# A hybrid attention and RWKV-7 block with experts: paired chunk products, later value products and row maxima by way of DRAM in the mixer stage

## The chip, the cores and the metric

The kernel runs on one core of a Trainium2 chip. Times are device microseconds of one execution; the time before is the median of three runs. A core has a matmul engine (TensorE, PE in the profile; its weight loads stand apart as PEld), VectorE (DVE), ScalarE (ACT), GpSimd (POOL) and SyncE (SP), which here issues nearly all transfers. PE writes its results to PSUM, which has eight banks of 512 fp32 per partition; DVE and ACT read them from there.

## The reference, cut to what matters

One encoder block over 2048 tokens of width 1024, in fp32:

```
p = rmsnorm(x) (modulated) @ w_in
o_att  = softmax(q k^T / 8) v      8 heads of 64 on 2 key/value heads, all 2048 keys
o_rwkv = for each direction, per token:
           sa = S (-kk);  S = S*w + sa (kk*a)^T + v k^T;  y = S r    8 heads, S is 64x64
x = x + gate * (concat(o_att, o_rwkv) @ w_out)
x = x + gate * (16 expert FFNs, each on its 256 best tokens)
```

The change is in the two token mixers alone, `o_att` and `o_rwkv`. In the attention each row of scores has its maximum subtracted before the exponential, and the weighted values are divided by the row's sum. RWKV's recurrence is computed in chunks of 64 tokens: for each head and chunk there are 64x64 products of the chunk's columns with each other, masked to one triangle; a triangular system is solved for them; and then the state is carried from chunk to chunk.

## The kernel before, in words

Four stages follow one another: the projections with their preparation, the mixers, the output projection with the router, and the experts. Instructions are issued in an order that is decided when the kernel is built: a scheduler simulates the engines, and at each moment takes the earliest instruction in program order that is ready; `high_priority` lets a block go ahead of what stands before it. On the chip each engine then keeps to its list, SP's transfers too: an instruction that must wait holds up everything behind it on its engine.

In the mixers (`mixers`) two generators are stepped in turn. `attention` goes through 16 blocks, a block being a pair of heads j and a quarter qc of 512 queries. Within a block (`att_out`) 16 key blocks of 128 follow each other: four matmuls give the scores of two heads (L694, L695) in the one two-bank buffer `st`, ACT takes the exponential (L696), DVE and POOL add it to the running sums (L699), and `values` multiplies it by the values (L686), the two heads side by side in the left and right 64 columns of the array. fp32 matmuls are two instructions each in the trace, fp32r ones one. At every second key block the value products of the two key blocks before it are issued at high priority. One step of a key block also takes three steps of `att_max` for the next block: 32 score tiles (L647, L648), reduced by DVE (L649) in two PSUM buffers `s`, then the maxima are split in a high and a low part (L654, L655), eight small matmuls with the identity turn them into rows (L660) and two ACT copies put them in rows 64 and 65 of the tile `qa` (L662), so that the score matmuls of that block subtract them. After a block `att_finish` sums over the partitions (L669), takes the reciprocal (L671) and multiplies.

`rwkv` goes through 16 groups (4 head pairs, 2 directions, 2 halves of the sequence), each of four quarters of four chunk pairs. For a quarter `rw_a1` loads a tile `xin` and, for each head, multiplies 64 rows of it by each other in four matmuls into one PSUM tile (L846); DVE masks the tile (L849); four transposes and an ACT copy follow (L854, L855), and two transfers bring the parts that the solve needs to DRAM (L857). These tiles all use PSUM bank `pa`, except that group 1 goes round `pa`, `pb` and `pc`. `rw_solve` loads the 32x32 diagonal blocks back (L867) and solves them in 30 dependent steps on DVE or POOL (L876, L878), writes them to DRAM (L886), and `rw_merge` joins them with matmuls (L915, L921). The recurrence itself (`rq_av`, `rq_wu`, `rq_l`, `rq_step`: L955 to L1011) uses banks `pb` and `pc`. In `rwkv` each quarter has four stations; `extra` runs at each of them and takes one step of `rw_a1` for the group after next, three of the solve, and one of the finish. A group's `rw_a1` has twelve steps, so that it ends with the third quarter of the group that runs.

Of the kernel before, what the change touches and what calls it, by code (L numbers as in the profile page):

```python
# [7 lines left out]
F32 = mybir.dt.float32  # L8
F32R = mybir.dt.float32r
# [580 lines left out]
class Attention(Encoder):  # L590
    def attention_pools(self, c):
# [9 lines left out]
        self.kl1 = self.a_k.tile([66, T], F32R, name="kl1")  # L601

# [19 lines left out]
    def att_max(self, j, qc, keys, res):  # L622
# [30 lines left out]
        hl = self.a_q.tile([P, 8, 2], F32R, tag="mhl", name="mhl")  # L653
        nc.vector.tensor_copy(out=hl[:, :, 0], in_=nm)  # L654
        nc.vector.tensor_tensor(out=hl[:, :, 1], in0=nm, in1=hl[:, :, 0].bitcast(F32), op=ALU.subtract)  # L655
        yield
        for h in range(2):
            pm = self.a_ps.tile([P, 512], F32, tag="s", name="m_ps", bufs=SB)
            for qt in range(4):
                nc.tensor.matmul(pm[64:66, qt * P : (qt + 1) * P], hl[:, 4 * h + qt, :].bitcast(F32), self.ident,  # L660
                                 start=True, stop=True, tile_position=(0, 64))
            nc.scalar.copy(out=q2[h][64:66, :], in_=pm[64:66, :])  # L662
            yield

    def att_finish(self, j, qc, av, acc):
# [5 lines left out]
        nc.vector.reciprocal(out=rec, in_=sm)  # L671
# [3 lines left out]
    def att_out(self, keys, v, q):  # L675
# [12 lines left out]
        for kb in range(16):  # L688
# [4 lines left out]
            for h in range(2):  # L693
                nc.tensor.matmul(s[:, h, :], khh[:, ks], qs[h], start=True, stop=False)  # L694
                nc.tensor.matmul(s[:, h, :], kl1[:, ks], q2[h], start=False, stop=True)  # L695
# [7 lines left out]
            if kb % 2 == 0 and kb:  # L703
                with self.tc.high_priority():
# [61 lines left out]
class Rwkv(Attention):  # L766
# [59 lines left out]
    def rw_a1(self, n, g):  # L826
# [5 lines left out]
        banks = cycle(("pa", "pb", "pc") if n == 1 else ("pa",))  # L832
        mask = self.masks[d]
        for i0, q in enumerate(range(4) if d == 0 else range(3, -1, -1)):
# [5 lines left out]
            rv = r56.rearrange("p c (x k) -> p c x k", k=64)  # L840
            for h in range(2):
                hs = slice(64 * h, 64 * h + 64)
                p1 = self.bank(next(banks)).tile([P, 4, P], F32, tag="p", name="p1")
                for i in range(4):
                    xr, u = X[hs, i // 2, :], i % 2
                    nc.tensor.matmul(p1[:, i, :].rearrange("p (x k) -> p x k", k=64), xr[:, 128 * u : 128 * u + 128],  # L846
                                     xr[:, 256:512].rearrange("p (x u k) -> p x u k", x=2, u=2)[:, :, u, :], start=True, stop=True)
                dst = rv[:, :, 0:3:2, :] if h == 0 else rv[:, :, 3:5, :]
                nc.vector.tensor_tensor(out=dst, in0=p1.rearrange("p c (x k) -> p c x k", k=64),  # L849
                                        in1=mask.unsqueeze(1).to_broadcast([P, 4, 2, 64]), op=ALU.mult)  # L850
                yield
# [763 lines left out]
```

## Time and profile before

| what | value |
|---|---|
| time, median of 3 runs | 3756.29 us (3753.66 to 3756.6) |
| the profiled execution's own time | 3751.49 us |
| its span from first to last instruction | 3749.8 us |
| PE busy over the span | 3509.9 us (94%) |
| DVE, ACT, POOL busy | 2516.7, 1755.2, 1512.5 us (67%, 47%, 40%) |
| granted PE clock, mean of the span | 0.957 of full |

The page gives shares over the whole span, in which the stages have different limits. The mixers alone fill PE from about 860 us to 2340 us; the projections lie before and the output projection, the router and the experts behind. "Busy" of PE contains modelled ends of matmuls, so that the distance from the start of one group of matmuls to the start of the next is the safer measure of what it costs.

### The profile page before, as it was taken

How to read it: one execution, taken by the hardware profiler on the slowest of the kernel's cores; microseconds unless marked ns; L12 is line 12 of the kernel's file. 1: busy time of each engine (PE TensorE's matmuls, PEld its weight loads, DVE VectorE, ACT ScalarE, POOL GpSimd, SP SyncE). 2: the span in 40 equal slices, each digit the busy share in tenths (PEclk: the TensorE clock that was granted, in tenths of full speed). 3: DMA queues.
4: the chain of work that ended last, by engine and by line, in shares of the span. 5: the costliest groups of instructions: out<-in, count | busy, mean ns of one | idle time of the engine just before them, and what ended most of it. 6: DMA issues, size and time to landing. Idle time of an engine off the chain costs nothing. (4 is left out here: it accounts for less than half of the span.)

```text
span 3749.8 us, 61495 instructions
## 1 busy us (share of the span) xinstructions
PE 3509.9 (94%) x23436; PEld 2856.7 (76%) x23436; DVE 2516.7 (67%) x4289; ACT 1755.2 (47%) x3066; POOL 1512.5 (40%) x1484
## 2 busy tenths in 40 slices
PE   6998899799999999999999997993999999999998
PEld 5887788656666666676666664772999999999997
DVE  6688778876857778558867675447555656655653
ACT  4445444414555555545555564231444444444443
POOL 3445344526263353663364554332332332322321
PEclk8999899879999999999999998996999999999999
DMA  5335334443323433433333232443566766767664
GB/s 182 105 130 168 112 113 141 139 129 73 91 68 79 121 95 85 114 88 87 84 85 85 69 82 82 156 145 113 188 206 205 222 202 216 218 203 222 220 199 127
DMA packets 531228, 510.93 MB, mean 136 GB/s; under 512 B 213304, under 2 KB 449954, under 8 KB 525812
## 3 DMA queue, kind: packets, MB, share of 16 engines
q1 hardware_dynamic: 520612, 472.08, 41.1%
q0 software_dynamic: 10000, 34.91, 4.0%
q8 instruction: 185, 3.03, 0.3%
q14 instruction: 111, 0.91, 0.1%
q10 hardware_dynamic: 320, 0.00, 0.0%
HBM read 392.57 MB, written 109.07 MB: 134 GB/s over the span
## 5 line engine op out<-in xcount | busy, mean ns | idle before, releaser
L1452 DVE TENSOR_TENSOR w_lo<-w_raw,w_hi 128x2048 fp32r<-128x2048 f32 x189 | 432.3, 2293 | 385.8 <-ACT w_hi L1449 385.4
L1516 PE MATMUL gu<-hh,w_lo 128*128 128x256 f32 x2048 | 573.5, 280 | 0.0
L1516 PE MATMUL gu<-hl,w_hi 128*128 128x256 f32 x2048 | 572.7, 280 | 0.0
L1516 PE MATMUL gu<-hh,w_hi 128*128 128x256 f32 x2048 | 572.5, 280 | 0.0
L699 POOL TENSOR_TENSOR acc<-acc,pt 128x512 f32<-128x512 f32 x256 | 354.9, 1391 | 469.0 <-ACT pt L696 456.0
L1449 ACT CAST w_hi<-w_raw 128x2048 fp32r<-128x2048 f32 x192 | 366.9, 1912 | 319.9 <-PE down L1539 133.3
L696 ACT ACTIVATE pt<-st_ps 128x1024 f32<-128x1024 f32 x256 | 262.2, 1024 | 394.8 <-PE st_ps L695 221.2
L649 DVE TENSOR_REDUCE mx<-s_ps 128x1 f32<-128x512 f32 x512 | 342.6, 681 | 149.7 <-PE s_ps L648 148.2
L247 PE MATMUL proj_ps<-hh,w_hi 128*128 128x258 f32 (+1 forms) x1280 | 375.3, 294 | 32.8 <-DVE s_k L265 23.8
L1516 PEld LDWEIGHTS gu<-hh,w_lo 128*128 128x128 f32 x2048 | 388.0, 189 | 0.0
L1516 PEld LDWEIGHTS gu<-hh,w_hi 128*128 128x128 f32 x2048 | 385.6, 188 | 1.3
L1516 PEld LDWEIGHTS gu<-hl,w_hi 128*128 128x128 f32 x2048 | 385.5, 188 | 1.4
L247 PE MATMUL proj_ps<-hl,w_hi 128*128 128x258 f32 (+1 forms) x1280 | 373.0, 292 | 6.4 <-DVE hl L149 5.9
L247 PE MATMUL proj_ps<-hh,w_lo 128*128 128x258 f32 (+1 forms) x1280 | 371.5, 290 | 0.0
L149 POOL TENSOR_TENSOR dl<-hid,dh 128x256 fp32r<-128x256 f32 x128 | 135.1, 1056 | 448.1 <-ACT dh L148 447.8
L686 PE MATMUL o_ps<-pt,av 128*64 128x512 f32 x1024 | 278.5, 627 | 6.7 <-ACT pt L696 6.7
L247 PEld LDWEIGHTS proj_ps<-hh,w_hi 128*128 128x128 f32 x1280 | 250.8, 196 | 41.7 <-issue 23.0
L247 PEld LDWEIGHTS proj_ps<-hl,w_hi 128*128 128x128 f32 x1280 | 251.4, 196 | 10.6 <-DVE hl L149 6.6
L699 DVE TENSOR_TENSOR acc<-acc,pt 128x512 f32<-128x512 f32 x192 | 194.7, 1014 | 91.0 <-ACT pt L696 90.3
L247 PEld LDWEIGHTS proj_ps<-hh,w_lo 128*128 128x128 f32 x1280 | 250.6, 196 | 2.1 <-issue 1.1
L647 PE MATMUL s_ps<-khh,qhl 128*128 128x512 f32 x512 | 240.6, 471 | 9.5 <-DVE mx L649 8.1
L694 PE MATMUL st_ps<-qhl,khh 128*128 128x512 f32 x512 | 229.0, 447 | 2.8 <-ACT pt L696 1.8
(418 smaller groups left out, 8125.1 us busy)
## 6 DMA issues: line engine op xcount, KB each, us to landing
w_raw<-in_w_gate_dram SPq DMA_DIRECT2D x64, 1024.0 KB
w_raw<-in_w_up_e_dram SPq DMA_DIRECT2D x64, 1024.0 KB
w_raw<-in_w_down_dram SPq DMA_DIRECT2D x64, 1024.0 KB
d_x<-X SPq DMA_DIRECT2D x32, 1024.0 KB
xin<-d_x SPq DMA_DIRECT2D x64, 512.0 KB
w_raw<-in_w_in_dram SPq DMA_DIRECT2D x80, 256.0 KB
mod_w<-in_w_ada_dram SPq DMA_DIRECT2D x64, 256.0 KB
mod_w<-in_w_ada_dram SPq DMA_DIRECT2D x8, 1024.0 KB
```

What stands on the lines that cost most here:

```text
L149: (eng or nc.gpsimd).tensor_tensor(out=lo, in0=src, in1=hi.bitcast(F32), op=ALU.subtract)
L247: nc.tensor.matmul(acc[:, :n], a[:, kt, :], b[:, kt, lo : lo + n], start=(kt == 0 and m == 0), stop=(kt == KT - 1 and m == 2))
L647: nc.tensor.matmul(s, qs[h][:, ts], khh[:, ks], start=True, stop=False)
L649: nc.vector.tensor_reduce(out=mx[:, 4 * h + qt, kc : kc + 1], in_=s, axis=AX.X, op=ALU.max)
L686: nc.tensor.matmul(av[64 * h : 64 * h + 64, :], v[:, kb, :], pt[:, h, :], start=(kb == 0), stop=(kb == 15), tile_position=(0, 64 * h))
L694: nc.tensor.matmul(s[:, h, :], khh[:, ks], qs[h], start=True, stop=False)
L696: nc.scalar.activation(out=pt, in_=s, func=AF.Exp, scale=0.125)
L699: eng.tensor_tensor(out=acc[:, h, :], in0=(first if kb == 1 else acc)[:, h, :], in1=pt[:, h, :], op=ALU.add)
L1449: nc.scalar.copy(out=hi, in_=raw)
L1452: eng.tensor_tensor(out=lo, in0=raw, in1=hi.bitcast(F32), op=ALU.subtract)
L1516: nc.tensor.matmul(acc[:, m, :], a[:, kt, i * P : (i + 1) * P], b[:, kt, :], start=(kt == 0 and n == 0), stop=(kt == KT - 1 and n == 2))
```

## The change

Six edits. In `rw_a1` the two heads' products go to two tiles in banks `pa` and `pb`, and the four matmuls of one head alternate with those of the other, each head's in its own half of the array's rows; masks, transposes and copies are as before, the step between the two heads is gone (so that a group has eight steps instead of twelve), and group 1 no longer uses `pc`. `extra` takes a step of `rw_a1` only at the third and fourth station of a quarter. In `att_out` the value products of two key blocks are ordered behind the last score matmul of the current key block. In `att_max` the split maxima of both heads are turned by one transpose of 16 columns, copied by ACT, written to DRAM, and read back by two transfers into rows 64 and 65 of the two `qa` tiles. In `att_finish` the reciprocal is taken in four parts of 128 columns. In the output projection a gap in SBUF is 512 bytes larger, which follows the new tile's size.

```diff
--- before.py
+++ after.py
@@ -599,6 +599,7 @@
         self.ones = self.a_k.tile([P, 64], F32, name="ones")
         self.nc.vector.memset(self.ones, 1.0)
         self.kl1 = self.a_k.tile([66, T], F32R, name="kl1")
+        self.d_m = self.dram.tile([4, 4, 2, 2, 512], F32, name="d_m")
 
     def att_keys(self, g):
 
@@ -650,17 +651,21 @@
                     yield
         nm = self.a_q.tile([P, 8], F32, tag="nm", name="nm")
         nc.vector.tensor_reduce(out=nm, in_=mx, axis=AX.X, op=ALU.max, negate=True)
-        hl = self.a_q.tile([P, 8, 2], F32R, tag="mhl", name="mhl")
-        nc.vector.tensor_copy(out=hl[:, :, 0], in_=nm)
-        nc.vector.tensor_tensor(out=hl[:, :, 1], in0=nm, in1=hl[:, :, 0].bitcast(F32), op=ALU.subtract)
+        hl = self.a_q.tile([P, 2, 2, 4], F32R, tag="mhl", name="mhl")
+        n3 = nm.rearrange("p (h t) -> p h t", h=2)
+        nc.vector.tensor_copy(out=hl[:, :, 0, :], in_=n3)
+        nc.vector.tensor_tensor(out=hl[:, :, 1, :], in0=n3, in1=hl[:, :, 0, :].bitcast(F32), op=ALU.subtract)
+        yield
+
+        pm = self.a_ps.tile([P, 512], F32, tag="s", name="m_ps", bufs=SB)
+        nc.tensor.transpose(pm[:16, :P], hl.bitcast(F32).rearrange("p h x t -> p (h x t)"), self.ident)
+        mt = self.a_q.tile([16, P], F32, tag="mt", name="mt", bufs=1)
+        nc.scalar.copy(out=mt, in_=pm[:16, :P])
+        nc.sync.dma_start(out=self.d_m[j, qc].rearrange("h x (t p) -> (h x t) p", p=P), in_=mt)
         yield
         for h in range(2):
-            pm = self.a_ps.tile([P, 512], F32, tag="s", name="m_ps", bufs=SB)
-            for qt in range(4):
-                nc.tensor.matmul(pm[64:66, qt * P : (qt + 1) * P], hl[:, 4 * h + qt, :].bitcast(F32), self.ident,
-                                 start=True, stop=True, tile_position=(0, 64))
-            nc.scalar.copy(out=q2[h][64:66, :], in_=pm[64:66, :])
-            yield
+            nc.sync.dma_start(out=q2[h][64:66, :].bitcast(F32), in_=self.d_m[j, qc, h])
+        yield
 
     def att_finish(self, j, qc, av, acc):
         nc = self.nc
@@ -668,7 +673,9 @@
         for h in range(2):
             nc.tensor.matmul(sm[64 * h : 64 * h + 64, :], self.ones[:, 0:64], acc[:, h, :], start=True, stop=True, tile_position=(0, 64 * h))
         rec = self.a_l.tile([P, 512], F32, tag="rec", name="rec")
-        nc.vector.reciprocal(out=rec, in_=sm)
+
+        for c in range(0, 512, P):
+            nc.vector.reciprocal(out=rec[:, c : c + P], in_=sm[:, c : c + P])
         nc.vector.tensor_tensor(out=rec, in0=av, in1=rec, op=ALU.mult)
         (nc.gpsimd if (j, qc) == (3, 3) else nc.sync).dma_start(out=self.d_o[j, :, qc * 512 : (qc + 1) * 512], in_=rec)
 
@@ -692,7 +699,7 @@
             s = self.o_ps.tile([P, 2, 512], F32, tag="st", name="st_ps", bufs=1)
             for h in range(2):
                 nc.tensor.matmul(s[:, h, :], khh[:, ks], qs[h], start=True, stop=False)
-                nc.tensor.matmul(s[:, h, :], kl1[:, ks], q2[h], start=False, stop=True)
+                st = nc.tensor.matmul(s[:, h, :], kl1[:, ks], q2[h], start=False, stop=True)
             nc.scalar.activation(out=pt, in_=s, func=AF.Exp, scale=0.125)
             if kb:
                 for h, eng in enumerate((nc.gpsimd if kb % 8 == 3 else nc.vector, nc.gpsimd)):
@@ -701,7 +708,7 @@
                 first = pt
 
             if kb % 2 == 0 and kb:
-                with self.tc.high_priority():
+                with self.tc.high_priority(), self.tc.issue_after(st.ins):
                     values(kb - 2)
                     values(kb - 1)
             if kb >= 6 and self.block in MOD_BLOCKS:
@@ -755,7 +762,7 @@
         self.att_finish(*done)
 
 
-from itertools import chain, cycle
+from itertools import chain
 
 GC = 16
 QB = 2
@@ -829,7 +836,6 @@
         ct, d, half = g["id"]
         c0 = half * GC
         g["r56"] = {}
-        banks = cycle(("pa", "pb", "pc") if n == 1 else ("pa",))
         mask = self.masks[d]
         for i0, q in enumerate(range(4) if d == 0 else range(3, -1, -1)):
             X = self.r_x.tile([P, 2, 512], F32, tag="xin", name="xin")
@@ -838,18 +844,20 @@
             r56 = self.r56_of(n, i0).tile([P, 4, 384], F32, tag="r56", name="r56")
             g["r56"][q] = r56
             rv = r56.rearrange("p c (x k) -> p c x k", k=64)
+
+            p1 = [self.bank(b).tile([P, 4, P], F32, tag="p", name="p1") for b in ("pa", "pb")]
+            for i in range(4):
+                for h in range(2):
+                    xr, u = X[64 * h : 64 * h + 64, i // 2, :], i % 2
+                    nc.tensor.matmul(p1[h][:, i, :].rearrange("p (x k) -> p x k", k=64), xr[:, 128 * u : 128 * u + 128],
+                                     xr[:, 256:512].rearrange("p (x u k) -> p x u k", x=2, u=2)[:, :, u, :], start=True, stop=True,
+                                     tile_position=(64 * h, 0))
             for h in range(2):
-                hs = slice(64 * h, 64 * h + 64)
-                p1 = self.bank(next(banks)).tile([P, 4, P], F32, tag="p", name="p1")
-                for i in range(4):
-                    xr, u = X[hs, i // 2, :], i % 2
-                    nc.tensor.matmul(p1[:, i, :].rearrange("p (x k) -> p x k", k=64), xr[:, 128 * u : 128 * u + 128],
-                                     xr[:, 256:512].rearrange("p (x u k) -> p x u k", x=2, u=2)[:, :, u, :], start=True, stop=True)
                 dst = rv[:, :, 0:3:2, :] if h == 0 else rv[:, :, 3:5, :]
-                nc.vector.tensor_tensor(out=dst, in0=p1.rearrange("p c (x k) -> p c x k", k=64),
+                nc.vector.tensor_tensor(out=dst, in0=p1[h].rearrange("p c (x k) -> p c x k", k=64),
                                         in1=mask.unsqueeze(1).to_broadcast([P, 4, 2, 64]), op=ALU.mult)
-                yield
-            p2 = self.bank(next(banks)).tile([P, 4, P], F32, tag="p", name="p2")
+            yield
+            p2 = self.bank("pa").tile([P, 4, P], F32, tag="p", name="p2")
             for i in range(4):
                 nc.tensor.transpose(p2[:, i, :], X[:, i // 2, 128 * (i % 2) : 128 * (i % 2) + 128], self.ident)
             nc.scalar.copy(out=rv[:, :, 1:6:4, :], in_=p2.rearrange("p c (x k) -> p c x k", k=64))
@@ -1108,8 +1116,10 @@
                     with self.tc.high_priority():
                         self.rq_step(prev, j)
 
-            def extra():
-                run(a1, 1)
+            def extra(j):
+
+                if j >= 2:
+                    run(a1, 1)
                 if k < 3:
                     run(solve, 3)
                 else:
@@ -1119,14 +1129,14 @@
 
             step(0)
             self.rq_l(Qs[i], 0)
-            extra()
+            extra(0)
             yield
             step(1)
             self.rq_l(Qs[i], 1)
-            extra()
+            extra(1)
             yield
             step(2)
-            extra()
+            extra(2)
             stage_load(i + 2)
             yield
             step(3)
@@ -1134,7 +1144,7 @@
                 fin = chain(fin, self.rq_done(prev, *quarters[i - 1]))
             if i + 2 < len(quarters):
                 self.rq_av(Qs[i + 2])
-            extra()
+            extra(3)
             if i + 1 < len(quarters):
                 if k == 3:
                     run(merge)
@@ -1215,7 +1225,7 @@
         pool = lambda name, bufs=1: c.enter_context(tc.tile_pool(name=name, bufs=bufs, reuse_waits="tile"))
         skip = lambda name, size: pool(name).tile([P, size // 4], F32, name=name)
         tp = pool("op_t", 2)
-        skip("op_gap0", 10240)
+        skip("op_gap0", 10240 + 512)
         wps = [pool("op_w0")]
         skip("op_gap1", 35840)
         wps.append(pool("op_w1"))
```

## Rows read from the trace of the kernel before

**Rows 1.** Mixers in seven stretches: header (busy us by engine, clock), and sum.

```profile
core 0: us, PE busy (x) PEld busy (x) DVE busy (x) ACT busy (x) POOL busy (x), PEclk, DMA share, GB/s
...
2060.00:2300.00 240.00, 229.27 (x1369) 153.46 (x1368) 168.20 (x263) 151.41 (x296) 128.57 (x139) 0.99 0.29 76
...
sum 1480.00, PE 1427.69 PEld 989.43 DVE 1048.90 ACT 814.33 POOL 745.73; mean PE 203.96 PEld 141.35 DVE 149.84 ACT 116.33 POOL 106.53
```

**Rows 2.** Waits of PE, 860 to 2340 us: waiter, releaser, total us, times, longest.

```profile
PE yT_ps L1056 <- DVE y L1051: 8.1, 1, 8.1
PE av_ps L961 <- DMA l<-d_v: 6.4, 6, 2.8
...
PEld st_ps L694 <- issue: 146.1, 177, 1.6
```

**Rows 3.** PE in order of time, mid-mixers: start us, duration us, line, operation.

```profile
1506.66 0.68 PE L961 MATMUL av_ps<-l,r 64*64 64x64 f32 x16
...
1507.51 1.08 PE L686 MATMUL o_ps<-pt,av 128*64 128x512 f32 x4 [0.17 <-ACT pt L696]
...
1508.52 0.50 PE L694 MATMUL st_ps<-qhl,khh 128*128 128x512 f32 x1
...
1508.86 0.40 PE L695 MATMUL st_ps<-qa,kl 66*128 66x512 f32 x1
...
1509.10 0.40 PE L694 MATMUL st_ps<-qhl,khh 128*128 128x512 f32 x1
...
1509.33 0.40 PE L695 MATMUL st_ps<-qa,kl 66*128 66x512 f32 x1
...
1509.66 1.16 PE L846 MATMUL p<-xin 64*128 64x128 f32 x8
...
1510.75 0.66 PE L999 MATMUL s_ps<-sr,lc 128*128 128x64 f32 x4
```

**Rows 4.** Groups of value products in time order: first, a double one, last.

```profile
860.46 1.08 PE L686 MATMUL o_ps<-pt,av 128*64 128x512 f32 x4
...
1500.55 1.94 PE L686 MATMUL o_ps<-pt,av 128*64 128x512 f32 x8
...
2328.73 1.08 PE L686 MATMUL o_ps<-pt,av 128*64 128x512 f32 x4 [0.16 <-ACT pt L696]
```

**Rows 5.** Groups of instructions, 860 to 2340 us: busy us, mean ns, idle before.

```profile
L846 PE MATMUL p<-xin 64*128 64x128 f32 x896 | 135.8, 290 | 2.2 <-DVE r L849 2.2
...
L849 DVE TENSOR_TENSOR r<-p,mask 128x512 f32<-128x512 f32 x112 | 76.2, 681 | 41.4 <-PE p L846 26.9 <-PE l_ps L983 13.8
```

**Rows 6.** Turn from one attention block to the next, in order of time.

```profile
1068.82 0.67 DVE L649 TENSOR_REDUCE mx<-s_ps 128x1 f32<-128x512 f32 x1
...
1070.72 1.02 ACT L696 ACTIVATE pt<-st_ps 128x1024 f32<-128x1024 f32 x1
...
1072.97 1.91 PE L660 MATMUL m_ps<-ident,mhl 128*2 128x128 f32 x16
...
1075.31 1.06 ACT L662 CAST qa<-m_ps 2x512 fp32r<-2x512 f32 x2
...
1080.79 3.36 DVE L671 RECIPROCAL rec<-sum_ps 128x512 f32<-128x512 f32 x1 [0.43 <-PE sum_ps L669]
...
1081.23 1.02 ACT L696 ACTIVATE pt<-st_ps 128x1024 f32<-128x1024 f32 x1 [2.53 <-PE st_ps L695]
```

**Rows 7.** Way of the solve through DRAM, and from its end to the merge.

```profile
1023.88 0.59 SPq L857 DMA_DIRECT2D d_a<-r  x1
...
1030.73 0.25 POOL L876 TENSOR_TENSOR ts_t<-ts 64x30 f32<-64x30 f32 x1 [1.36 <-DMA ts<-d_a]
...
1617.14 1.01 SPq L886 DMA_DIRECT2D d_r<-ts  x2
...
1633.82 1.76 PE L915 MATMUL z_ps<-bdr,bdn 128*128 128x128 f32 x8
```

**Rows 8.** SP's waits, 860 to 2340 us, the longest in total.

```profile
SPq L942 <- DVE mx L649: 131.6, 29, 11.8
```

**Rows 9.** Value products near the end, when attention runs nearly alone.

```profile
2298.18 1.08 PE L686 MATMUL o_ps<-pt,av 128*64 128x512 f32 x4 [1.17 <-ACT pt L696]
```

**Rows 10.** One matmul group of every quarter: min/median/max ns, first and last start.

```profile
L971 PE MATMUL wu_ps<-r,tt x512: 270/275/527, 872.2 to 2264.3; 128*128 128x128 f32 x171
```

## The prediction

> **What bounds the kernel now.** I read the page's row of 40 slices first: PE has nine tenths or more nearly everywhere, so an edit to the mixers counts only if it takes work or gaps from PE there, or if it starves PE. Next the busy times by stretch, from 860 to 2340 us, where both mixer streams run. PE is busy 1427.7 of 1480 us, at a clock close to full; DVE 1048.9 (71%), ACT 814.3, POOL 745.7 [rows 1]. Then the waits: the longest that PE has on another engine in these 1480 us are 8.1 and 6.4 us [rows 2]. The reader is to see that PE is full: while one stream waits, the other's matmuls stand in its list. The mixers' time is therefore the sum of what PE's groups cost from start to start, and that is read from PE in order of time [rows 3]. The third row of the waits (146.1 us, 177 times) is no free time: it is the stretch in which no weights can be loaded because value products run in the halves of the array.
>
> What a group costs beside its products shows there. From score matmul to score matmul PE takes 0.24 us (1509.10 to 1509.33), into a group of another tiling 0.33 (1509.33 to 1509.66), and the first score matmul after value products takes 0.34 (1508.52 to 1508.86). So each change of tiling costs 0.09 us before it and about 0.10 after it.
>
> **Part 1, chunk products.** A group of eight instructions (one head) takes 1.09 us to the next group (1509.66 to 1510.75), with its entry 1.18 [rows 3]. The stretch holds 896 instructions [rows 5], 56 pairs of groups; the other 8 pairs lie before 860 us, where PE has holes, and I count nothing for them. After the change a pair is one group of sixteen. No row shows the array's upper and lower half at work together; the left and right half are shown. Four instructions of 512 columns take 1.01 us (1507.51 to 1508.52) [rows 3]; an instruction of 128 columns takes 1.09/8 = 0.136, so four times the columns alone would make 4 x 0.54 = 2.2. They go in pairs. The bounds of the pair are thus 2.36 us as now, less one entry and the end of one group (together some 0.2), and 1.18 with full overlap. I take full overlap, as the rows of the other halves are nearest: 56 x 1.18 = 66 us less PE time; the other end is 56 x 0.2 = 11.
>
> The Trainium skill, page "TensorE: Matmul & The Clock Gate", section on packing small matmuls, has a measured 3.07 times for four row tiles; at that share of the ideal the pair would cost about 0.3 us more, and the term would be some 50 instead of 66, an estimate that no run here shows.
>
> Masking remains 112 DVE instructions of 0.681 us [rows 5], two per pair. Both tiles now wait for DVE at once, 1.36 us, and the transposes want bank `pa`, the recurrence bank `pb`. Today DVE's masking delays these groups by 2.2 us in all [rows 5], as other work lies between. Since a step of `rw_a1` is now a whole station long, I cost this at nothing; without that cover it is 1.36 - 1.18 = 0.18 us per pair, 10 us.
>
> The Trainium skill's page "TensorEngine Tiling (Array Packing)", under "PSUM Bottleneck", says that tiling makes TensorE faster but not the emptying of PSUM; by that rule the 10 us would fall due, and the term would be 56.
>
> **Part 2, value products.** From the first to the last group [rows 4] I count 227 groups with 984 recorded instructions: the two key blocks that the code issues together mostly come apart, four instructions each, since the second waits for its exponential. Behind the current scores both are ready; 984/8 = 123 groups should remain, 104 fewer. Each saves an entry (0.09), a slow first score (0.10) and the end of a group: two single ones of 1.08 us against a double one of 1.94, 0.22 [rows 3, 4]. That is 0.41; as ends are modelled I take 0.35: 104 x 0.35 = 36 us. Bounds: 0, if the planner still parts them, and 43. What is moved is four matmuls per key block past four score matmuls on PE; behind them wait only later scores, which wait for the exponential anyway. The buffers `pt` are three, and the next exponential but one needs the oldest: it comes free before.
>
> There is a gain off PE too: near the end, where attention runs nearly alone, PE waits 1.17 us for each exponential, then has 1.01 us of value products before the next scores can start [rows 9]. In the new order these run under the exponential. For the eight or so key blocks there I take 5 us, bounds 0 and 8.
>
> **Part 3, maxima.** Per block sixteen instructions, 1.91 us [rows 6], become one transpose of a single 128-column instruction (0.14 at 0.136 each) without change of tiling: 16 x 1.75 = 28 us less PE. ACT has one copy instead of two (1.06 us for both). But the way is longer. Now it is 1072.97 to 1076.37, 3.4 us [rows 6]. The new one is transpose and copy, some 1 us, and then a write and a read of DRAM on SP, one after the other. The nearest row is the solve's: from its last write's issue at 1023.88 to the first use of what was read at 1030.73, 6.85 us, with far more and smaller pieces [rows 7]. Lower bound: the issue times of one write and two reads alone, at 0.59 each, 1.8. So a block's turn gets between -0.6 and +4.5 us; I take 4.5, 72 us over 16 blocks. The next block's scores wait for that, and so does attention: from its last maximum at 1068.82 to the first exponential of the next block at 1081.23 it already takes 12.4 us [rows 6]. RWKV's matmuls fill this: PE's waits stay under 10 us each [rows 2]. I charge 10 of the 72 us. Without the cover it is all 72. Behind the waiting transfers on SP stand RWKV's loads, requested two quarters ahead.
>
> The Trainium skill, page "DMA: Bandwidth & Descriptors", on the anatomy of one DMA, gives about 2.0 us fixed per transfer on the gpsimd path; two in a row would be 4.0 instead of 6.85, an estimate, and the charge 4 instead of 10. No row here has transfers of 2 KB rows from end to end.
>
> **Part 4, later steps of `rw_a1`.** Eight steps, two per quarter, end with the group's fourth quarter instead of its third. A quarter is (2264.3 - 872.2)/63 = 22.1 us [rows 10]. The solve starts as soon as the last write has landed, so it starts about 22 us later. What stands between its end and the merge is at its shortest 1617.14 + 1.01 to 1633.82, 15.7 us [rows 7], and that has to hold another way through DRAM. So in the tightest groups the merge comes late by 22.1 - 15.7 = 6 us, up to 6.4 + 6.85 = 13 if nothing of the gap was slack; I count four groups of fifteen with a gap under 23 us. That is 25 to 52 us of RWKV's latency, which attention's matmuls cover; I charge 10.
>
> **Part 5, reciprocal, gap.** Four parts instead of one of 3.36 us [rows 6]: the same 3.36 or up to four starts more (about 0.2 us each at the shortest DVE steps), and other DVE work can go between. Nothing, 16 x 0.8 = 13 us of DVE at most. The larger gap in SBUF moves no work.
>
> **Sum.** PE loses 66 + 36 + 28 = 130 us; tail 5. Back come 10 (DRAM way) and 10 (later solve). With PE's load down by 9%, the share of DVE rises from 71% to about 1049/1365 = 77%, and holes that are now filled open: PE's idle 52 us in the stretch [rows 1] I let grow by 20. Net 130 + 5 - 40 = 95. The profiled execution's 3751.5 becomes 3656.5; the median of the runs shown is 4.8 above it, so 3661.
>
> **Rivals.**
> A: the upper and lower half do not overlap. Against it: the other halves do; for it: no row. The term is 11 instead of 66: 3661 + 55 = 3716.
> B: RWKV's chain takes over, since solve and merge come late and PE runs dry with less to fill: all of 52 us uncovered instead of 10, 3703. For it: 15.7 against 22.1 us; against it: attention has work left at each turn.
> C, slower: the maxima hang on SP. SP issues in order, and it has stood waiting at one line 29 times, 131.6 us, up to 11.8 at once [rows 8]. If the write of the maxima stands behind such a wait, a turn grows by 4.5 + 11.8 = 16.3 us; with half of it uncovered, 16 x 8.15 = 130 us in place of the 10 charged: 3781. It decides from (95 + 10)/16 = 6.6 us uncovered per block. Against it: PE has so far found work in turns of 12.4 us.
> D: A and B together, 3758: no change.
>
> **How the numbers follow.** Forecast 0.63, with its own range of 3620 to 3695 (the part-2 and part-3 bounds); A 0.10; B 0.11; C 0.10; D 0.06. Faster by over 0.2%, about what a measurement of this kernel can tell from no change, are the forecast, A and B: 0.84. D is same: 0.06. C is slower: 0.10. The range 3620 to 3735 leaves out C, D and a thin end below.
>
> **What would show it.** Value products in groups of eight, some 123 of them in the mixers; sixteen chunk-product instructions within about 1.1 us with starts in pairs, not 2.0; no group of 1.9 us for maxima; the mixers ending near 2245 instead of 2340 us. The turn from last maximum to next exponential should read 15 to 17 us while PE's waits there stay small: long PE waits on a transfer into `qa` mean C; waits at the merge or at the masks of the solve mean B. It is wrong if PE's groups shrink as said and the mixers still end after 2300 us.

## The result, and the profile after

The changed kernel took 3879.35 us (median of 4 runs, 3874.2 to 3886.54) against 3756.44 us for the kernel before on the same chip: a ratio of 1.0328, with a 95% interval of 1.0309 to 1.0347. It is 123 us slower; the forecast was 95 us faster.

First the profile page after: TensorE (PE) still shows eight or nine tenths in most slices, and the granted clock falls to six tenths in slices 14 and 21, in the mixers.

```profile
span 3876.5 us, 61049 instructions
...
PE   7997999889998899899979998897699999999998
...
PEclk8999999789999698899869998898799999999999
```

The stretches of [rows 1] after (us, PE busy, PEld, DVE, ACT, POOL, clock, DMA). Two of them run at 0.83 and 0.80 of the full clock, and the mixers now take some 1600 us.

```profile
1100.00:1340.00 240.00, 213.02 (x1179) 157.36 (x1179) 156.78 (x294) 114.68 (x245) 89.14 (x94) 0.83 0.35 89
...
1820.00:2060.00 240.00, 211.70 (x1174) 159.04 (x1172) 144.84 (x274) 108.55 (x231) 66.09 (x68) 0.80 0.32 78
2060.00:2300.00 240.00, 229.96 (x1341) 158.38 (x1339) 171.19 (x276) 125.20 (x244) 126.21 (x142) 0.96 0.30 73
...
sum 1600.00, PE 1466.40 PEld 1032.79 DVE 1045.84 ACT 804.30 POOL 750.73; mean PE 209.49 PEld 147.54 DVE 149.41 ACT 114.90 POOL 107.25
```

PE's waits after, 860 to 2460 us, against [rows 2]. The longest is 33.8 us at the recurrence's step (`rq_step`), which waits for `lc`, the sum that VectorE makes from `rq_l`'s bank. The wait for the maxima's transfer into `qa` is small.

```profile
PE s_ps L1007 <- DVE lc L994: 33.8, 23, 3.7
PE s_ps L648 <- DVE mx L650: 15.9, 24, 1.8
PE p L862 <- DVE r L857: 9.8, 9, 4.0
PE st_ps L702 <- DMA qa<-d_m: 8.4, 8, 2.5
```

The same step in the kernel before:

```profile
PE s_ps L999 <- DVE lc L986: 3.5, 6, 1.5
```

The matmul of every quarter, as in [rows 10]. Its last start moves from 2264.3 to 2421.7: a quarter takes (2421.7 - 871.9)/63 = 24.60 us instead of 22.10. Over 63 quarters that is 158 us. The span grew by 127, since attention has less left to do alone at the end: its last exponential came 63 us after the last `wu_ps` before and comes 6 us after it now.

```profile
L979 PE MATMUL wu_ps<-r,tt x512: 271/275/580, 871.9 to 2421.7; 128*128 128x128 f32 x171
```

The last exponential, before and after:

```profile
2327.66 1.02 ACT L696 ACTIVATE pt<-st_ps 128x1024 f32<-128x1024 f32 x1
...
2427.33 1.02 ACT L703 ACTIVATE pt<-st_ps 128x1024 f32<-128x1024 f32 x1 [0.40 <-PE st_ps L702]
```

What was meant to become cheaper on PE did so in part. In order of time: a chunk-product group of eight (one head, 1.08 us to the next group, 1.09 before, [rows 3]) and a value group of eight.

```profile
1153.99 1.16 PE L852 MATMUL p<-xin 64*128 64x128 f32 x8
1155.07 0.50 PE L701 MATMUL st_ps<-qhl,khh 128*128 128x512 f32 x1
...
1156.21 1.94 PE L693 MATMUL o_ps<-pt,av 128*64 128x512 f32 x8
```

The two heads do not alternate. Their banks come free at different times, and the planner issues one head's four products as soon as that head's bank is free; only 3 groups hold both heads, and all three lie ahead of the mixers' 860 us. Value products stand in 147 groups where 227 stood.

Where the new time lies is seen best in one passage through the bank `pb`, about 1280 us (start, duration, line; TensorE at half clock). The tiles pass through it one at a time: the second `l_ps` (read by ACT and then DVE until 1283.43), then the second head's chunk products at 1284.11, which the mask has read at 1286.91, and only then `av_ps` at 1287.02 and `wu_ps` at 1289.54, which the next step of the recurrence needs. From the last read of `l_ps` to `av_ps` it is 3.6 us.

```profile
1279.79 2.02 PE L991 MATMUL l_ps<-r,l 128*128 128x128 f32 x8
...
1281.85 0.58 ACT L993 COPY lc<-l_ps 64x512 f32<-64x512 f32 x1 [3.31 <-PE l_ps L991]
...
1282.74 0.69 DVE L994 TENSOR_TENSOR lc<-l_ps,ri 64x512 f32<-64x512 f32 x1
...
1284.11 2.07 PE L852 MATMUL p<-xin 64*128 64x128 f32 x8
...
1286.22 0.69 DVE L857 TENSOR_TENSOR r<-p,mask 128x512 f32<-128x512 f32 x1 [0.64 <-PE p L852]
...
1287.02 0.64 PE L963 MATMUL av_ps<-ident,al 128*128 128x128 f32 x2
...
1289.54 2.02 PE L979 MATMUL wu_ps<-r,tt 128*128 128x128 f32 x8
```

In the kernel before no tile stands between `l_ps` and `av_ps`. One of its passages, 0.33 us from the last read to `av_ps`:

```profile
1414.64 0.89 PE L983 MATMUL l_ps<-r,l 128*128 128x128 f32 x6
...
1419.24 0.69 DVE L986 TENSOR_TENSOR lc<-l_ps,ri 64x512 f32<-64x512 f32 x1
...
1420.26 0.39 PE L955 MATMUL av_ps<-ident,al 128*128 128x128 f32 x2
...
1427.66 1.05 PE L971 MATMUL wu_ps<-r,tt 128*128 128x128 f32 x8
```

In the kernel before I followed all tiles of that bank from the first matmul to the last instruction that reads it: 252 tiles in 1394 us, four to a quarter (`av`, `wu`, two `l`), unread products in it 62% of the time. Averaged over all quarters, the way from the second `l` to the next `wu` takes 11.8 us before and 14.6 after. Inside it, the stretch from the last read of the second `l` to the start of `av` grows from 1.5 to 5.9 us on average, and the rest shrinks by some 1.5. In the changed kernel 56 quarters have a tile of products there: 1.9 us pass until its matmuls start, it is held for 2.8, and `av` starts 1.8 later.

### The profile page after: what moved, and what is told of

It is laid out like the page before. It is cut to its first block, busy times and chain, and to the rows that moved or that the text cites. A ratio compares the mean times of both kernels' runs of the same rounds, so it can differ in the third digit from the quotient of the medians.

```text
span 3876.5 us, 61049 instructions
## 1 busy us (share of the span) xinstructions
PE 3551.2 (92%) x23196; PEld 2903.2 (75%) x23196; DVE 2515.1 (65%) x4337; ACT 1747.0 (45%) x3050; POOL 1520.4 (39%) x1484
## 5 line engine op out<-in xcount | busy, mean ns | idle before, releaser
L706 POOL TENSOR_TENSOR acc<-acc,pt 128x512 f32<-128x512 f32 x256 | 362.7, 1421 | 386.8 <-ACT pt L703 365.0
L693 PE MATMUL o_ps<-pt,av 128*64 128x512 f32 x1024 | 268.8, 632 | 1.2 <-ACT pt L703 1.1
L1007 PEld LDWEIGHTS s_ps<-sr,lc 128*128 128x128 f32 x1024 | 167.1, 213 | 124.4 <-DVE lc L994 49.2
L1011 ACT ACTIVATE sr<-s_ps,pc 64x64 f32<-64x64 f32 x512 | 158.3, 309 | 223.9 <-PE s_ps L1007 215.5
L706 DVE TENSOR_TENSOR acc<-acc,pt 128x512 f32<-128x512 f32 x192 | 174.7, 910 | 120.6 <-ACT pt L703 115.1
```

The costliest lines, as they stand in the source:

```text
L693: nc.tensor.matmul(av[64 * h : 64 * h + 64, :], v[:, kb, :], pt[:, h, :], start=(kb == 0), stop=(kb == 15), tile_position=(0, 64 * h))
L706: eng.tensor_tensor(out=acc[:, h, :], in0=(first if kb == 1 else acc)[:, h, :], in1=pt[:, h, :], op=ALU.add)
L1007: nc.tensor.matmul(p6[:, c, h, :], lc[:, c, h, :], s0[:, h, :], start=True, stop=True)
L1011: nc.scalar.activation(out=s1[ks, h, :], in_=p6[ks, c, h, :], func=AF.Copy, scale=pc)
```

## The experiments

Eighteen kernels ran; each ratio is to the kernel before on the same chip. "Quarter" is worked out from the row of `wu_ps` as above, in the one execution that was profiled; e2's was its longest of six (3787.3 us).

| run | edit | us | ratio [95%] | quarter, us |
|---|---|---|---|---|
| | before | 3756.4 | 1 | 22.10 |
| | changed | 3879.4 | 1.0328 [1.0309, 1.0347] | 24.60 |
| e1 | changed, steps earlier | 3812.0 | 1.0177 [1.0149, 1.0204] | 23.47 |
| e2 | before, steps late | 3769.1 | 1.0058 [1.0037, 1.0079] | 23.23 |
| e3 | changed without part 1 | 3762.5 | 1.0038 [1.0017, 1.0059] | 22.40 |
| e4 | before, maxima alone | 3785.7 | 1.0116 [1.0081, 1.0151] | 22.58 |
| e5 | changed, modulation moved | 3880.6 | 1.0349 [1.0318, 1.0379] | 24.69 |
| e6 | e1, heads forced to alternate | 3853.6 | 1.0266 [1.0225, 1.0307] | 24.18 |
| e7 | e1, one bank | 3779.7 | 1.0073 [1.0052, 1.0095] | 22.62 |
| e8 | before, values alone | 3742.9 | 0.9984 [0.9967, 1.0000] | 22.21 |
| e9 | before, part 1 alone | 3850.1 | 1.0243 [1.0218, 1.0267] | 24.15 |
| e10 | changed, one bank | 3792.0 | 1.0088 [1.0066, 1.0110] | 23.09 |
| e11 | e4, old matmuls kept | 3786.2 | 1.0076 [1.0054, 1.0099] | 22.58 |
| e12 | before, values, reciprocal | 3764.8 | 1.0007 [0.9993, 1.0021] | 22.53 |
| e13 | e10, bank `pb` claimed once more | 3906.6 | 1.0427 [1.0396, 1.0458] | 25.00 |
| e14 | changed, banks swapped | 3857.9 | 1.0314 [1.0281, 1.0346] | 23.90 |
| e15 | before, second head in `pb` | 3865.8 | 1.0336 [1.0304, 1.0368] | 24.29 |
| e16 | before, values, modulation moved | 3750.2 | 1.0004 [0.9989, 1.0020] | 22.61 |
| e17 | changed, `av` to bank `pa` | 3763.1 | 1.0018 [1.0003, 1.0033] | 22.35 |
| e18 | e1, `av` to bank `pa` | 3813.3 | 1.0142 [1.0116, 1.0168] | 23.08 |

### e1 to e4: which part

My first theory was part 4: the later steps of `rw_a1` make RWKV's groups late. Its main rival (theory 2) was the second bank, and the third theory the maxima's way through DRAM.

e1_steps_earlier:
```
-                if j >= 2:
+                if k == 0 or j in (1, 2):
```


> The changed kernel, but the eight steps of rw_a1 are taken earlier: at every station of a group's first quarter, and at the second and third station of the others, so that they end with the third quarter, as before the change. Theory 1 (the last step of rw_a1 now ends with the fourth quarter, so that loading back, solve, merge and wu all have to fit in one group's time, and this cycle of some 100 us per group became the bound): most of the loss comes back, 3720 to 3780 us, wu-to-wu per group back under 93 us. Theory 2 (the products' second tile in bank pb delays the recurrence): 3850 to 3890, wu-to-wu still about 98. Theory 3 (the maxima's way through DRAM on SP): 3850 to 3890 as well.

Measured 1.0177: about half of the loss comes back, between the expectations.

e2_before_steps_late (before's twelve steps at the last three stations of each quarter):
```
-                run(a1, 1)
+                if j >= 1:
+                    run(a1, 1)
```


> The kernel before, nothing changed but that a step of rw_a1 is taken at three of a quarter's four stations instead of all, so that its twelve steps end with the fourth quarter instead of the third. Theory 1 (late end of rw_a1): 3820 to 3890 us, wu-to-wu per group 95 to 100 us against 90. Theories 2 (bank pb) and 3 (maxima through DRAM): no change, 3745 to 3770.

Measured 1.0058, a miss for theory 1: late steps alone cost 22 us, not the loss.

e3_products_undone (the changed kernel with `rw_a1` and `extra` of before):


> The changed kernel with rw_a1 and extra as they were before; value products, maxima and reciprocal stay changed. Theories 1 and 2 (the fault is in part 1): at or below the kernel before, 3690 to 3760 us, since the value products stand in 150 groups instead of 237 and the maxima cost 28 us less of PE. Theory 3 (maxima through DRAM): 3840 to 3890.

Measured 1.0038. Part 1 is worth 1.0328 - 1.0038 = 2.9%, some 109 us.

e4_maxima_only (before, with the new way of the maxima):


> The kernel before with the maxima alone changed (one transpose, DRAM, two transfers back). Theories 1 and 2: 3725 to 3765 us, the 28 us of PE work less against a turn that is up to 4.5 us longer. Theory 3: 3830 to 3890, with PE's waits on the transfer into qa as the longest.

Measured 1.0116, a miss for all three theories: the maxima's part alone makes the kernel slower, though it takes the 1.9 us of PE per block away.

### e5 to e8: what stalls, and the halves

Attention stands still in blocks 5 and 11, from first to last exponential 162 and 171 us instead of 111 and 79. By the code and the order in the trace, `att_finish` waits there for its tile `rec`, held by the modulation's sum, which waits for tiles held by RWKV's late finish.

e5_mod_blocks_moved:
```
-MOD_BLOCKS = (0, 2, 4, 5, 6, 9, 10, 13)
+MOD_BLOCKS = (0, 1, 2, 5, 6, 9, 12, 13)
```


> The changed kernel with the side work of the modulation (mod_rest) taken in blocks 1 and 12 instead of 4 and 10, so that its tiles, which share buffers with RWKV's finish, no longer stand between that finish and attention. Theory 4 (attention runs ahead, then stands in blocks 5 and 11 until RWKV's finish gives the shared buffers back, and PE falls to half clock there): block lengths 164 and 173 us fall below 110, the granted clock of the mixers rises, 3770 to 3830 us. Theory 1 in its strict form (RWKV's own cycle is the bound, the standing is only its sign): blocks 5 and 11 shorten but the last group's wu stays near 2370 us and the time at 3855 to 3890.

Measured 1.0349. Blocks 5 and 11 shrink to 82 and 76 us, block 13 grows from 77 to 162, and the time stays. A stall of that length only moves to another block: where attention stands does not set the time. A kernel without the stall was not run.

e6_halves_forced (e1, each chunk product ordered behind the one before it, so that heads alternate):
```
+                    if last is not None: order.enter_context(self.tc.issue_after(last))
```


> e1 (steps earlier) with each chunk-product matmul ordered behind the one before it, so that the two heads alternate, now in nearly all of the 64 pairs (in the changed kernel as built, the planner set one head's four before the other's in most). If the upper and lower half of the array overlap: sixteen instructions in about 1.1 us, 55 us less PE time than e1, 3750 to 3795 us against e1's 3812. If they do not: sixteen in about 2.0 us and 3795 to 3830.

Measured 1.0266, slower than e1. On PE in order of time the halves do work together: fourteen instructions (seven products; the first went ahead alone) in the 1.16 us in which eight ran before. By the starts of the single instructions, the two of a pair in this group start 7 ns apart or less and most pairs follow each other by 0.11 us, which is also the step from one instruction to the next in a group of one head.

```profile
1118.18 1.16 PE L854 MATMUL p<-xin 64*128 64x128 f32 x14
```

So rival A is wrong about the array, and the saving is no saving of time. Why it costs against e1 was not tested; both banks are then taken at once.

e7_one_bank (e1, heads one after the other in `pa`):
```
-            p1 = [self.bank(b).tile(...) for b in ("pa", "pb")]
+                p1 = self.bank("pa").tile(...)
```


> e1 (steps earlier, eight steps) with the two heads' products one after the other in bank pa alone, as before the change. Theory 2 (the second tile in bank pb delays the recurrence, which e1 has left): near e3, 3750 to 3780 us. If bank pb costs nothing: as e1, 3795 to 3825.

Measured 1.0073 against e1's 1.0177: the second bank costs here too.

e8_values_only (before, with the value products ordered behind the scores):
```
+                with self.tc.high_priority(), self.tc.issue_after(st.ins):
```


> The kernel before with the value products alone ordered behind the current scores; by the built list they then stand in 156 groups instead of 237. By PE work alone: 81 groups at 0.35 us = 28 us less, 3715 to 3735. If the faster attention only runs ahead of RWKV and then stands in blocks 5 and 11: 3740 to 3775, with block 5 over 130 us (113 before).

Measured 0.9984, some 6 us of the 41 forecast, though the number of value groups falls as in the changed kernel.

### e9 to e12: alone and without

e9_products_alone:


> The kernel before with only the first part of the change (two banks, eight steps, the last two stations of each quarter). Theory 1 (that part alone makes the loss, by the late steps and the held bank; the change without it stands 14 us over before, so it is worth 3879 - 3763 = 117): 3850 to 3880 us, RWKV's last group near 2355. Rival (the parts cost only together, as the maxima and the value products also lengthen RWKV's cycle): 3785 to 3835. My forecast's own theory: 3680 to 3700.

Measured 3850.1 us, ratio 1.0243: 91 us. Part 1 alone makes three quarters of the loss.

e10_late_one_bank (the changed kernel, `p1` as in e7):


> The changed kernel with both heads' tiles in the first bank, one after the other, and its late steps as they are. Theory 1 (late steps cost 67 and the second bank 32, each by itself): 3879 - 32 = 3835 to 3860. Theory 2 (the second bank is what makes late steps dear, since they fall where the recurrence needs it): 3770 to 3800, near the kernel with early steps and one bank (3780).

Measured 1.0088, as theory 2 said. With e1 and e7 this makes a square: late or early steps differ by 1.5% with two banks (1.0328, 1.0177) and by 0.15% with one (1.0088, 1.0073). Late steps are dear with the second bank; with one they cost 6 us here and 22 in e2.

e11_old_maxima_kept:
```
+            for qt in range(4):
+                nc.tensor.matmul(old[64:66, qt * P : (qt + 1) * P], hl[:, h, :, qt].bitcast(F32), self.ident, ...)
```


> Before with the maxima's new path alone, and the eight old matmuls of each block issued beside it with their results unread: about 28 us of TensorE's work is back. If the loss of the maxima's part (37 us) is that TensorE, with less to do at the turn, runs more stretches at half clock: 3745 to 3775. If the loss is the new path itself (its trip through DRAM, the queue it holds), the old work comes on top: 3795 to 3820.

Measured 3786.2 us, between the two expectations; by the ratio (1.0076 against e4's 1.0116) the old matmuls, 28 us of PE work, came back for nothing or less. The turn from last maximum to first exponential is 15.2 us here against 12.7 in e4, so that a longer turn alone does not make the loss either. The mean granted clock of e4 and of e11 (span, clock; before: 3749.8 us at 0.957):

```profile
core 0: 3774.1 us, clock 0.948
```

```profile
core 0: 3780.6 us, clock 0.955
```

In e4 the stretch 1100 to 1220 us is PE-busy and runs at 0.86, where before had 0.99 (e4 first, then before).

```profile
1100.00:1220.00 120.00, 116.95 (x625) 80.60 (x625) 85.73 (x155) 57.66 (x117) 42.09 (x33) 0.86 0.27 66
...
1100.00:1220.00 120.00, 116.94 (x716) 82.06 (x714) 90.26 (x170) 66.59 (x135) 46.54 (x39) 0.99 0.30 73
```

e12_values_reciprocal:
```
+        for c in range(0, 512, P):
+            nc.vector.reciprocal(out=rec[:, c : c + P], in_=sm[:, c : c + P])
```


> The kernel before with the value products behind the next scores and the reciprocal in parts, without the chunk products and the maxima. If RWKV's cycle is the bound and neither touches it, both give next to nothing: 3735 to 3748, just faster than both kernels. If the reciprocal's four instructions delay the additions on VectorE: 3750 to 3765.

Measured 3764.8 us, in the range for delayed additions; but before took 3758.6 on this chip, and the ratio, 1.0007 [0.9993, 1.0021], tells no change. With e8's 0.9984 the parts of the reciprocal give nothing and may cost some us.

### e13 to e18: what of the bank

e13_bank_claimed (e10, one product more per quarter, in `pb`):
```
+            hold = self.bank("pb").tile([P, 4, P], F32, tag="p", name="hold")
+            nc.tensor.matmul(hold[:, 0, :]..., start=True, stop=True)
+            nc.vector.tensor_tensor(out=rv[:, 0, 3, 0:1], in0=hold[:, 0, 0:1], in1=mask[:, 0, 0:1], op=ALU.mult)
```


> The kernel of late steps and one bank, with one more claim of the second bank in each quarter of each group: one chunk product of the second head is computed once more there and one column of it masked once more into the place where it stands already. By itself that is 64 matmuls at 0.11 us and 64 small VectorE instructions, under 10 us. If the second bank's extra tenant is what costs (in the changed kernel 90 us more than with one bank): 3835 to 3880. If it was the work inside the tile or the pairing of the heads: 3785 to 3810.

Measured 1.0427, by the ratios 127 us above e10, more than expected. The claim is held 1.7 us on average in the mixers, and yet the quarter grows from 23.09 to 25.00 us. One of them in order of time: the claim is read at 1102.03, and the next tile starts at 1104.61. The bank is free in between; PE goes through other matmuls of its list.

```profile
1101.33 0.49 PE L860 MATMUL hold<-xin 64*128 64x128 f32 x2
...
1101.88 0.15 DVE L862 TENSOR_TENSOR r<-hold,mask 128x1 f32<-128x1 f32 x1
...
1104.61 0.38 PE L967 MATMUL av_ps<-ident,al 128*128 128x128 f32 x2
```

e14_banks_swapped:
```
-for b in ("pa", "pb")]
+for b in ("pb", "pa")]
```


> The changed kernel with the first head in the second bank and the second head in the first, so that the shared bank is freed by the first of the two masks. If the time for which the tile holds the bank is the cost: 3830 to 3865. If the number of turns in the bank is, or the late steps alone: 3870 to 3890, as the changed kernel.

Measured 3857.9 us, which lies in the range given for the hold; but before ran at 3747.4 on this chip, and the ratio, 1.0314, is the changed kernel's within the intervals. The edit does not shorten the hold: the products' tile is held for 2.8 us on average, as in the changed kernel. So the question of the hold stays open here.

e15_before_second_bank:
```
-                p1 = self.bank(next(banks)).tile(...)
+                p1 = self.bank(next(banks) if n == 1 else ("pa", "pb")[h]).tile(...)
```


> The kernel before with one edit: in groups 2 to 15 the second head's chunk products take the second bank (the twelve early steps, the maxima and all else as before). If the second bank alone costs: 3785 to 3840. If it costs only where the steps come late: 3745 to 3770. My forecast charged nothing for it: 3757.

The line also takes group 0, whose products lie ahead of 860 us. Measured 1.0336, above the range given for the second bank alone: this one edit to the kernel before, with its early steps and no other part, costs as much as the whole change.

```profile
L971 PE MATMUL wu_ps<-r,tt x512: 272/275/580, 877.8 to 2407.8; 128*128 128x128 f32 x171
```

e16_values_mod_moved (both edits shown above):


> The kernel before with the value products behind the next scores and the modulation's blocks moved from 4 and 10 to 1 and 12, as a version that might beat both. If RWKV's cycle is the bound, moving the modulation gives nothing: 3740 to 3755. If the long block 5 (113 us before, with the modulation in it) binds by itself: 3715 to 3735.

Measured 1.0004: block 5 shrinks from 111 to 78 us and nothing is won, so that block 5 does not bind. That RWKV's cycle binds in the kernel before does not follow: the quarter is 22.61 us here against 22.10, at the same time.

e17_changed_av_moved:
```
-        p3 = self.bank("pb").tile([P, 2, 4, 64], F32, tag="p", name="av_ps")
+        p3 = self.bank("pa").tile([P, 2, 4, 64], F32, tag="p", name="av_ps")
```


> The changed kernel with one edit: the RWKV group's four av tiles move from the second bank to the first. Theory of turns: one tile at a time passes through the second bank, 252 of them in 1394 us before (5.5 us each, 16 to a group, 88 us a group); the change makes it 20, about 105 us a group at its own 5.1 us; with av moved it is 16 again, and the first bank goes from 13 to 17 as it had before: 3745 to 3800. Rival (a chunk product's tile among the recurrence's, waiting for its mask, is the cost, however many tiles): 3845 to 3885.

Measured 1.0018: moving one other tile out of the bank gives 116 of the 123 us back, with chunk products in `pb` and steps late as in the changed kernel. Its quarter is 22.35 us, near before's 22.10, and the stretch from `l` to `av` is 1.7 us again.

```profile
L979 PE MATMUL wu_ps<-r,tt x512: 272/275/580, 876.8 to 2284.8; 128*128 128x128 f32 x171
```

e18_early_av_moved (e1 and e17's edit):


> The changed kernel with its steps earlier and av's tiles in the first bank: a version that might beat both. Theory of turns: 16 in the second bank, and no wait for late solves: 3725 to 3775. Rival: near the one with earlier steps alone, 3800 to 3820.

Measured 1.0142, a miss for the theory: with early steps the move gives back little, though the count of turns is e17's. In the trace the loss lies in the first quarter of each group, at whose four stations e1's edit puts four of the eight steps: it takes 29.8 us on average (22.3 before, 23.4 in e17), the other three 20.6, 19.5 and 23.3. So the count of tiles in a bank does not price a change by itself. Why that quarter is so long was not tested. No version beat the kernel before by more than e8's 0.16%, whose interval ends at no change.

## Why the prediction was wrong

**The step that failed is in part 1**: "Both tiles now wait for DVE at once ... the recurrence bank `pb` ... I cost this at nothing; without that cover it is 1.36 - 1.18 = 0.18 us per pair, 10 us." I priced VectorE's time for the masks. What fell due was a fifth tile in each quarter of a bank that the recurrence passes through one tile at a time: 24.29 - 22.10 = 2.2 us per quarter (e15), 25.00 - 23.09 = 1.9 (e13) and 24.60 - 22.35 = 2.25 (changed against e17), times 63 quarters 120 to 140 us. The term of 0 to 10 us is 118 (e15). The price depends on where the steps come: with the eight steps of the change, the second bank costs 24.60 - 23.09 = 1.5 us when they are late (against e10) and 23.47 - 22.62 = 0.85 when they are early (e1 against e7). It comes without the pairing of heads too (e15), and from a single product held for 1.7 us (e13). It goes when another tile leaves the bank in e17, but not in e18.

What is shown is thus that the claim of the bank makes the loss. What makes one claim so dear is open in part: of the stretch that grows, the hold is 2.8 us, and some 3.7 us lie before and behind it. In the passage of e13 shown above PE spends the time behind it on other matmuls of its list. The planner makes a new list for each edit, and no run kept the list while it changed the bank.

**What bounds the kernel** was misread before that. "PE is full" held for the busy column, and from it followed that each microsecond taken from PE counts. It does not: e8's fewer groups gave 6 us, e4 has 28 us less PE work and is slower, and e11 took that work back at no cost. I had the quarter of 22.1 us in hand [rows 10] and used it as a clock for part 4. In the changed kernel it sets the pace, since attention ends 6 us after the last `wu_ps`; every run with a quarter of 23 us or more is slower, by 0.6 to 4.3%, and e17 brings quarter and time back together. For the kernel before it is not shown that the quarter is the bound: attention runs on for 63 us behind the last `wu_ps`, e12 and e16 lengthen the quarter by 0.4 and 0.5 us at no more time, and no run made it shorter. TensorE's busy column stayed high, 1466 of 1600 us, as the work spread out, with some of it at half clock.

**Part 1's gain** of 66 us did not come, although the halves overlap (e6). The kernel before had shown it already, where I wrote that no row does: in its groups at 787.96 and 793.73 us two of these instructions start 6 ns apart, as the pairs of e6 do. The planner does not let the heads meet, which I had not asked: each head's bank is free at another time.

The Trainium skill, page "TensorE: Matmul & The Clock Gate", section "Measured speedup vs the span model", has 3.07 for four row tiles. The two tiles in e6 come nearer to their ideal of 2 than that does to 4.

The Trainium skill's page "Perfetto Trace Analysis", section "Matmuls", advises to let independent matmul groups rotate through different banks. Here that rule alone (e15) costs 3.4%: the other bank was not free, and the measurement decides. The section "Optimization Strategy" of the Trainium skill's page "Perfetto Trace Analysis" says that the same gap repeating on the engine that should be saturated can mean too little PSUM for the next tile. The 23 waits for `lc` repeat in that way, but each ends with VectorE's sum and not with a bank's release, so that no row here shows this cause.

**Part 2**: 147 groups, not 123; 36 + 5 us forecast, 6 measured alone (e8, 0 to 12 by its interval). **Part 3**: the PE work went; the turn from last maximum to first exponential grew from 10.2 to 13.4 us on average (15 to 17 forecast, from a row of 12.4 that was longer than the average). The way through DRAM took 3.4 us from the write's issue to the first use in a case with one other transfer between (1647.30 to 1650.68), against 6.85 taken from the solve:

```profile
1647.03 0.25 ACT L663 COPY mt<-m_ps 16x128 f32<-16x128 f32 x1
1647.30 0.33 SPq L664 DMA_DIRECT2D d_m<-mt  x1
...
1649.06 0.73 SPq L667 DMA_DIRECT2D qa<-d_m  x2
...
1650.68 0.50 PE L702 MATMUL st_ps<-qa,kl 66*128 66x512 f32 x1 [0.18 <-DMA qa<-d_m]
```

Net 18 us forecast (28 less 10), 37 lost by e4's medians and 43 by its ratio. The products taken away were worth nothing (e11), so the loss is not PE's work, and e11's turn is longer still at no more time. What makes it, SP's queue, the fallen clock or the new list, stays open. **Part 4**: charged 10; 22 alone (e2), 6 with one bank (e7, e10), 57 with two. **Part 5**: nothing, as forecast, or a few us lost (e12 against e8).

**Rivals.** B named the right chain, RWKV's, but by the merge and the solve, and still priced it as a gain. C named the maxima, which do cost time alone (e4), but by PE's wait for `qa`, which is 8.4 us in all. A was wrong about the array (e6), and yet the products cost PE what they cost before, since the heads do not meet. The test set at the end ("PE's groups shrink as said and the mixers still end after 2300 us") came out in its second half: the groups shrank in part, and the last exponential of attention moves from 2327.7 to 2427.3.

## What to carry to other kernels

Before a tile is given another PSUM bank, list who passes through that bank now, in order, and whether a recurrence is among them: here a turn of 0.85 to 2.25 us in each of 63 cycles outweighed every saving on a TensorE that looked full. A period that repeats, like the 22.1 us here, is a candidate for the bound; ask of each part of a change whether it lengthens or shortens that period. And test whether TensorE's work binds by taking some away: here that bought 6 us or nothing.

## What the runs showed of the hardware

In the changed kernel and in e4, which give TensorE less work, the granted clock was lower. The mean granted clock fell from 0.957 to 0.929 in the changed kernel; in the stretch below, where attention stands still and TensorE has RWKV's small matmuls alone and waits between them, it is 0.53 and 0.56 of 2.4 GHz, so nearly all of it is at 1.2. PE reads as 82 and 85% busy there. In e11, with the old products kept beside the new ones, the clock was 0.955 where e4 had 0.948. That the clock, and not the waits, makes part of the loss is argued from these rows; no run held the clock alone.

```profile
1260.00:1320.00 60.00, 49.17 (x245) 43.27 (x244) 35.02 (x82) 22.74 (x58) 7.94 (x7) 0.53 0.44 119
1920.00:1980.00 60.00, 51.16 (x261) 45.33 (x260) 15.11 (x32) 24.11 (x59) 5.37 (x7) 0.56 0.29 68
```
